# One gate product of a two-layer encoder from seven quarter products instead of eight

## The chip, the cores and the metric

The kernel runs on one core of a Trainium2 chip. A core has five engines with queues of their own: TensorE (PE in the profile, with its weight loads on a row of their own, PEld), VectorE (DVE), ScalarE (ACT), GpSimd (POOL) and SyncE (SP), which here only issues DMAs. The metric is the device time of one execution in microseconds, lower is better. Before the change it is 667.46 us, the median of three runs (667.1 to 667.55).

## The reference

The reference is an encoder trunk of two layers over 512 tokens with 1024 features, all in float32. Each layer has a token mixer, and after it the step that the change touches:

```python
h = x + y                                                     # y: output of the mixer
gate = jax.nn.sigmoid(rmsnorm(h, ple_norm[i]) @ ple_w_gate[i])  # (512x1024) @ (1024x1024)
x = h + gate * (p[i] @ ple_w_proj[i])
...
return rmsnorm(x, final_norm)                                 # after the second layer
```

Layer 0 mixes by neighbourhood attention, layer 1 by multi-head latent attention (MLA). `ple_norm` is scaled up by about 100, so the sigmoid's argument is large and small errors of the product can be seen in the output.

## The kernel before

**Precision.** No float32 matmul is used. Every operand is split in two: `hi`, a copy rounded to the matmul's type float32r (one ACT instruction), and `lo = x - hi` (one DVE or POOL instruction). A product is then the sum of three, hi by hi, lo by hi and hi by lo, all accumulated in one bank of PSUM (`mms`, `by_chunk`, L98 and L389). Activations are split by `split` (L87: ACT copy, DVE subtract), weights by `load_w` (L68: DMA from SP's queue into `wraw`, ACT copy into `whi` on L78, POOL subtract into `wlo` on L79).

**Tiling.** The 512 tokens are four blocks `t` of 128. A square product (1024 by 1024) is done in eight groups: two halves `n` of 512 output columns, and in each the four token blocks. One group is 24 matmuls of 128x128 by 128x512: eight slices of the contraction, three terms each. The weights of a half come as four chunks of 128x1024, each of which holds two slices.

**The second layer's last two products.** `out_proj` (L397) multiplies the attention's output `oT` by `mla_o`. DVE adds each group onto the residual rows `res[t]` (L409) and calls `turn_h` (L836): DVE multiplies the new half row by `ple_norm` (L839, `hg`), PE transposes it (L128), `split` makes `hnT[t]`, and after the second half ACT squares the row, DVE and POOL turn the sum into `rh[t]`, the inverse root mean square (L110 to L112). `gate_phase` (L465) multiplies `hnT` by the gate weights. Per group: ACT takes the sigmoid with `rh[t]` as its scale (L479), DVE multiplies by `pe` (L480; `pe` was computed earlier and is loaded from DRAM) and adds to `res[t]` (L482). `done` (L864) then gathers the sum of squares of the final norm, and in the half n = 0 POOL multiplies the row by the final gain (L879). When a row is complete, POOL raises to the power -1/2 (L882), DVE and ACT scale the two halves (L883, L884) and two DMAs write the row out. The very last group is done in two pieces of 256 columns.

**What sets the order.** The program is traced in the order of the source. A planner then puts each engine's instructions in order, the earlier in the source first among those that it takes to be ready, and hands out the buffers; the queues run in that order. So an instruction far down in the source can be queued early when its inputs are early, and one whose buffer is not free cannot. The buffers that matter here: three each of `wraw`, `whi` and `wlo`; five more pairs `whi`, `wlo` for the output and the gate product (`wxn` of L826); eight big buffers of 128x2048 (four hold `oT` until the output product is over, the other four `hnT`); two PSUM banks `mm`, two `S`, three `T`, one `O`; eight buffers `z` of 128x512, free once the attention is over; three of `pe`.

```python
    def load_w(self, ap, n, extra=False, parts=1, rest=None, late=None):   # L68
...
            nc.scalar.activation(hi[:, c], raw[:, c], AF.Copy)             # L78
            f = lambda e, c=c: e.tensor_tensor(out=lo[:, c], in0=raw[:, c], in1=hi[:, c].bitcast(F32), op=ALU.subtract)
```

Of the kernel before, what the change touches and what calls it, by code (L numbers as in the profile page):

```python
# [28 lines left out]
NWARM = 11  # L29
NLATE = 3  # L30
NEARLY = 7


def win(t, r0, r1, off, dims):
# [5 lines left out]
class Trunk:  # L40
    def __init__(self, tc, ctx, a, dbg=None):
        self.tc, self.nc, self.a = tc, tc.nc, a
        self.dbg = dbg or {}
        nc = self.nc
        ec = ctx.enter_context
        self.const = ec(tc.tile_pool(name="const", bufs=1))
        self.big = ec(tc.tile_pool(name="big", bufs=8))
        self.zp = ec(tc.tile_pool(name="zp", bufs=8))
        self.wp = ec(tc.tile_pool(name="wp", bufs=4))
        self.ps = ec(tc.tile_pool(name="ps", bufs=2, space=PSUM))  # L50
        self.ident = self.const.tile([P, P], F32, name="ident")
        self.half = self.const.tile([P, 1], F32, name="half")
        nc.vector.memset(self.half, -0.5)
        self.small = ec(tc.tile_pool(name="small", bufs=8))
        self.wx, self.wxn = None, 0
# [12 lines left out]
    def load_w(self, ap, n, extra=False, parts=1, rest=None, late=None):  # L68

        nc = self.nc  # L70
        pool = self.wx if extra else self.wp
        raw = self.wp.tile([P, 1024], F32, name="wraw", tag="wraw", bufs=3)
        hi = pool.tile([P, n if extra else 1024], F32R, name="whi", tag="whi", bufs=self.wxn if extra else 3)
        lo = pool.tile([P, n if extra else 1024], F32R, name="wlo", tag="wlo", bufs=self.wxn if extra else 3)
        w = n // parts
        for c in [slice(i * w, (i + 1) * w) for i in range(parts)]:
            nc.sync.dma_start(raw[:, c], ap[:, c])
            nc.scalar.activation(hi[:, c], raw[:, c], AF.Copy)  # L78
            f = lambda e, c=c: e.tensor_tensor(out=lo[:, c], in0=raw[:, c], in1=hi[:, c].bitcast(F32), op=ALU.subtract)  # L79
# [23 lines left out]
        return last  # L103


    def inv_rms(self, scratch, src, n):
# [4 lines left out]
        nc.vector.tensor_scalar(ss, ss, 1.0 / n, EPS, op0=ALU.mult, op1=ALU.add)  # L111
        nc.gpsimd.tensor_tensor(out=rs, in0=ss, in1=self.half, op=ALU.pow)  # L112
        return rs

    def rms(self, dst, src, g, n):
        rs = self.inv_rms(dst, src, n)
        self.nc.vector.scalar_tensor_tensor(dst, src, rs, g, op0=ALU.mult, op1=ALU.mult)

    def bcast(self, pool, ap, n, name, tag=None, bufs=None):
# [363 lines left out]
                    after(t, n, o, w)  # L483


    def mla_c(self, pool, xT, cT, sets):
        nc, a = self.nc, self.a
        tok = pool.tile([P, NT, 2, 16], F32, name="tok", tag="tok", bufs=1)
# [271 lines left out]
    def run(self):  # L760
# [7 lines left out]
        with tc.tile_pool(name="pre", bufs=4, reuse_waits="tile") as pool:  # L768
# [34 lines left out]
                nc.scalar.activation(xt[t], xt[t], AF.Square, accum_out=ss[:, t:t + 1])  # L803
            self.ple(pool, 0, "pe", 6, operands)
            nc.gpsimd.tensor_scalar(ss, ss, 1.0 / D, EPS, op0=ALU.mult, op1=ALU.add)
            nc.gpsimd.tensor_tensor(out=ss, in0=ss, in1=self.half.to_broadcast([P, NT]), op=ALU.pow)
            turned = self.transposes([ss[:, t:t + 1].to_broadcast([P, P]) for t in range(NT)])
            R = pool.tile([P, S], F32, name="R", bufs=1)
# [14 lines left out]
        x1T = None  # L823
        for layer in range(2):
            with tc.tile_pool(name=f"out{layer}", bufs=4, reuse_waits="tile") as pool:
                self.wx, self.wxn = pool, 5  # L826
                res = []
                for t in range(NT):
                    r = pool.tile([P, D], F32, name="r", tag="r")
                    nc.sync.dma_start(r, a["x"][t] if layer == 0 else self.spill[t])  # L830
                    res.append(r)
                gp = self.bcast(pool, a["ple_norm"][layer], D, "gp")
                gn = self.bcast(pool, a["norm_g"][1] if layer == 0 else a["final_norm"], D, "gn")
                hnT, rh = {}, {}

                def turn_h(t, n):  # L836

                    hg = pool.tile([P, S], F32, name="hg", tag="hg", bufs=3)
                    nc.vector.tensor_tensor(out=hg, in0=res[t][:, n * S:(n + 1) * S],  # L839
                                            in1=gp[:, n * S:(n + 1) * S], op=ALU.mult)  # L840
                    if n == 0:
                        hnT[t] = self.big.tile([P, 2 * KD, P], F32R, name="hnT", tag="big")
                    ps = self.transposes([hg[:, i * P:(i + 1) * P] for i in range(4)])
                    self.split(hnT[t][:, 4 * n:4 * n + 4, :], hnT[t][:, KD + 4 * n:KD + 4 * n + 4, :],
                               ps.rearrange("p (a b) -> p a b", a=4))
                    if n == 1:
                        sq = pool.tile([P, D], F32, name="sq", tag="xn", bufs=2)
                        rh[t] = self.inv_rms(sq, res[t], D)

                self.out_proj(a["na_o"] if layer == 0 else a["mla_o"], oT, res, turn_h, last)  # L850
                if layer == 0:
                    x1T = ([self.bigtile(f"x1h{g}") for g in range(2)], [self.bigtile(f"x1l{g}") for g in range(2)])

                    def done(t, n, o, w):
                        if n == 0:
# [3 lines left out]
                        self.rms(xn, res[t], gn, D)  # L859
                        self.rows_to_cols(xn, colsT(x1T, t))  # L860
                else:
                    mean = {}

                    def done(t, n, o, w):  # L864
                        c = slice(n * S + o, n * S + o + w)
                        r = res[t]
                        sq = pool.tile([P, D], F32, name="sq", tag="xn", bufs=2)
                        mn = self.small.tile([P, 1], F32, name="mn", tag="mn")
                        if c.start > S:
                            nc.vector.tensor_tensor_reduce(sq[:, :w], r[:, c], r[:, c], 1.0 / D, mean[t], op0=ALU.mult,  # L870
                                                           op1=ALU.add, accum_out=mn)
                        else:
                            ss = self.small.tile([P, 1], F32, name="ss", tag="ss")
                            nc.scalar.activation(sq[:, :w], r[:, c], AF.Square, accum_out=ss)
                            nc.vector.tensor_scalar(mn, ss, 1.0 / D, mean.get(t, EPS), op0=ALU.mult, op1=ALU.add)
                        mean[t] = mn
                        if c.stop < D:
                            if n == 0:
                                nc.gpsimd.tensor_tensor(out=r[:, c], in0=r[:, c], in1=gn[:, c], op=ALU.mult)  # L879
                            return  # L880
                        rs = self.small.tile([P, 1], F32, name="rs", tag="rs")
                        nc.gpsimd.tensor_tensor(out=rs, in0=mn, in1=self.half, op=ALU.pow)  # L882
                        nc.vector.scalar_tensor_tensor(r[:, S:], r[:, S:], rs, gn[:, S:], op0=ALU.mult, op1=ALU.mult)  # L883
                        nc.scalar.activation(r[:, :S], r[:, :S], AF.Copy, scale=rs)  # L884
                        nc.sync.dma_start(a["out"][t][:, S:], r[:, S:])
                        (nc.scalar if c.start > S else nc.sync).dma_start(a["out"][t][:, :S], r[:, :S])
                self.gate_phase(pool, layer, hnT, rh, res, done)
# [112 lines left out]
```

## Time and profile before

| | us |
|---|---|
| median of three runs | 667.46 |
| the profiled execution's span | 665.9 |
| what lies around the span, by the median | 1.6 |
| last weight split of the output product ends (POOL) | 596.1 |
| first matmul of the second gate | 614.1 |
| last matmul of the second gate ends | 658.6 |
| last instruction on DVE and ACT ends | 661.9 |

Times of the trace are counted from the start of the span. A row of the timeline gives start, duration, engine, line, operation, output and inputs; a row of the groups gives how many there are, their busy time, the mean duration in ns, and the idle time of the engine before them with what ended it. The profiled execution is the one that the prediction's sums are made against; its span and 1.6 us around it make the time of a run.

### The profile page before, as it was taken

What the parts mean: (1) busy time and instruction counts of PE and PEld (TensorE: products, weight loads), DVE (VectorE), ACT (ScalarE), POOL (GpSimd) and SP (SyncE); (2) the same over time, 40 slices, a digit from 0 to 9 for tenths busy, and PEclk for the clock granted to TensorE, in tenths of its full rate; (3) what the DMA queues carried; (4) which work ended last, traced back from release to release, by engine and by line L of the source; (5) the groups of instructions that cost most, each with busy time, mean ns of one, the idle gap of its engine ahead of it and who ended that gap; (6) DMA issues with size and microseconds to landing.
All of it is one profiled execution on the core that took longest, in us unless ns stands there. A gap on an engine that the chain in (4) does not pass through costs nothing.

```text
span 665.9 us, 9961 instructions
## 1 busy us (share of the span) xinstructions
PE 657.4 (99%) x3467; PEld 560.1 (84%) x3467; DVE 354.8 (53%) x794; ACT 407.9 (61%) x812; POOL 392.8 (59%) x320
## 2 busy tenths in 40 slices
PE   9999999999999999999999999999999999999995
PEld 6888888988988888888899888888888888888885
DVE  6280365736645514544625614888988875145234
ACT  7572586857767742543433635898979887436423
POOL 0395466575575765943044626786959786858410
PEclk9999999999999999999999999999999999999999
DMA  9944223222142236534233335120201223664022
GB/s 327 340 153 136 95 87 94 83 85 99 55 150 76 64 133 262 189 105 138 100 104 110 107 89 168 32 74 24 75 23 64 64 96 111 234 240 159 32 80 95
DMA packets 32386, 79.09 MB, mean 119 GB/s; under 512 B 4177, under 2 KB 8785, under 8 KB 32337
## 3 DMA queue, kind: packets, MB, share of 16 engines
q1 hardware_dynamic: 31904, 77.68, 35.0%
q10 hardware_dynamic: 432, 0.79, 0.3%
q8 instruction: 27, 0.44, 0.3%
q14 instruction: 23, 0.18, 0.1%
HBM read 66.92 MB, written 8.39 MB: 113 GB/s over the span
## 4 chain that ended last, share of the span: by engine, by line
PE 95%; DMA 1%; issue 1%; POOL 1%; DVE 0%; ACT 0%; SPq 0%; POOLq 0%; ACTq 0%
PE ps_mm L102 47%; PE ps_S L102 13%; PE ps_mm L550 6%; PE ps_T L128 6%; PE ps_O L661 4%; PE ps_T L102 3%; PE ps_O L102 3%; PE ps_T L227 2%; PE ps_O L383 2%; PE ps_mm L173 2%; PE ps_T L371 2%; PE ps_S L336 1%; PE ps_S L335 1%; PE ps_O L227 1%; DMA qe<-rl 1%
## 5 line engine op out<-in xcount | busy, mean ns | idle before, releaser
L79 POOL TENSOR_TENSOR wlo<-wraw,whi 128x1024 fp32r<-128x1024 f32 (+5 forms) x106 | 208.2, 1980 | 119.2 <-ACT whi L78 91.2
L78 ACT ACTIVATE whi<-wraw 128x1024 fp32r<-128x1024 f32 (+5 forms) x107 | 92.5, 886 | 86.9 <-PE ps_mm L102 17.8
L646 POOL TENSOR_TENSOR ex<-ex,rc 128x512 f32<-128x512 f32 x64 | 66.2, 1044 | 25.2 <-DVE rc L645 18.1
L102 PE MATMUL ps_mm<-whi,hnT 128*128 128x512 f32 (+1 forms) x272 | 70.2, 378 | 0.0
L102 PEld LDWEIGHTS ps_mm<-whi,hnT 128*128 128x128 f32 x272 | 49.3, 188 | 9.2
L644 ACT ACTIVATE ex<-ps_S,mx 128x512 f32<-128x512 f32 x64 | 44.0, 688 | 11.9 <-DVE mx L642 10.8
L642 DVE TENSOR_REDUCE mx<-ps_S 128x1 f32<-128x512 f32 x64 | 43.7, 683 | 6.9 <-PE ps_S L102 6.2
L91 DVE TENSOR_TENSOR pt_lo<-ps_T,pt_hi 128x512 fp32r<-128x512 f32 x64 | 43.3, 682 | 7.7 <-ACT pt_hi L89 7.3
L358 POOL TENSOR_TENSOR ex<-ex,rc 128x128 f32<-128x128 f32 (+1 forms) x64 | 34.1, 561 | 20.9 <-DVE rc L354 20.9
L102 PE MATMUL ps_mm<-xh,whi 128*128 128x512 f32 x152 | 40.8, 399 | 0.0
L102 PE MATMUL ps_mm<-wlo,hnT 128*128 128x512 f32 (+1 forms) x136 | 40.5, 378 | 0.0
L89 ACT ACTIVATE pt_hi<-ps_T 128x512 fp32r<-128x512 f32 x64 | 37.7, 594 | 4.4 <-PE ps_T L128 4.1
L128 PE MATMUL ps_T<-ident,ex 128*128 128x128 f32 x256 | 38.4, 272 | 0.0
L102 PE MATMUL ps_mm<-xl,whi 128*128 128x512 f32 x152 | 38.2, 390 | 0.0
L102 PE MATMUL ps_mm<-xh,wlo 128*128 128x512 f32 x152 | 38.0, 390 | 0.0
L128 PEld LDWEIGHTS ps_T<-ident,ex 128*128 128x128 f32 x256 | 31.5, 140 | 7.7 <-POOL ex L646 0.4
L102 PEld LDWEIGHTS ps_mm<-xl,whi 128*128 128x128 f32 x152 | 28.4, 188 | 5.8
L102 PEld LDWEIGHTS ps_mm<-xh,wlo 128*128 128x128 f32 x152 | 28.3, 188 | 5.8
L194 DVE TENSOR_TENSOR u<-ps_O,u 64x512 f32<-64x512 f32 x32 | 22.0, 687 | 19.9 <-ACT u L193 19.3
L112 POOL TENSOR_TENSOR rs<-ss,half 128x1 f32<-128x1 f32 x20 | 12.7, 637 | 33.7 <-DVE ss L111 33.6
L480 DVE TENSOR_TENSOR sg<-pe,sg 128x512 f32<-128x512 f32 (+1 forms) x17 | 12.4, 728 | 35.8 <-ACT sg L479 35.8
L352 ACT ACTIVATE ex<-ex,mx 128x128 f32<-128x128 f32 (+1 forms) x64 | 30.3, 474 | 1.9 <-DVE mx L342 1.0
(354 smaller groups left out, 1644.6 us busy)
## 6 DMA issues: line engine op xcount, KB each, us to landing
pe<-pe SPq DMA_DIRECT2D x32, 256.0 KB, 2.8
wraw<-na_qk SPq DMA_DIRECT2D x16, 512.0 KB, 3.3
wraw<-gate SPq DMA_DIRECT2D x16, 512.0 KB, 3.4
wraw<-na_v SPq DMA_DIRECT2D x8, 512.0 KB, 3.3
wraw<-na_o SPq DMA_DIRECT2D x8, 512.0 KB, 3.5
wraw<-mla_z SPq DMA_DIRECT2D x8, 512.0 KB, 3.5
wraw<-mla_o SPq DMA_DIRECT2D x8, 512.0 KB, 3.6
wraw<-na_z SPq DMA_DIRECT2D x6, 512.0 KB, 5.4
```

Source lines behind the costliest of these rows:

```text
L78: nc.scalar.activation(hi[:, c], raw[:, c], AF.Copy)
L79: f = lambda e, c=c: e.tensor_tensor(out=lo[:, c], in0=raw[:, c], in1=hi[:, c].bitcast(F32), op=ALU.subtract)
L89: self.last_copy = nc.scalar.activation(hi, src, AF.Copy, scale=scale)
L91: nc.vector.tensor_tensor(out=lo, in0=src, in1=hi.bitcast(F32), op=ALU.subtract)
L102: last = self.last_mm = nc.tensor.matmul(out, l, r, start=i == 0, stop=i == n - 1)
L128: self.last_mm = self.nc.tensor.transpose(t[:, i * P:(i + 1) * P], b, self.ident)
L352: self.last_exp = nc.scalar.activation(e, e, AF.Exp, scale=-1.0, bias=mx[:, qt:qt + 1], accum_out=sm[:, qt:qt + 1])
L358: nc.gpsimd.tensor_tensor(out=e, in0=e, in1=rc[:, qt:qt + 1].to_broadcast([P, e.shape[1]]), op=ALU.mult)
L550: self.last_mm = nc.tensor.matmul(PS[key], *terms[i], start=i == 0, stop=i == len(terms) - 1)
L642: nc.vector.reduce_max(mx, sp, axis=AX.X, negate=True)
L644: nc.scalar.activation(ex, sp, AF.Exp, bias=mx, accum_out=sm)
L646: nc.gpsimd.tensor_tensor(out=ex, in0=ex, in1=rc.to_broadcast([P, S]), op=ALU.mult)
```

## The change

In layer 1 the gate product is no longer made in eight groups of 24 matmuls. The 512x1024 matrix of activations is taken as four quarters (two token blocks by 512 features) A11, A12, A21, A22, and the weights as four quarters of 512x512, `E` and `F` (slices 0 to 3; left and right columns), `G` and `H` (slices 4 to 7). Seven products of sums of quarters stand for the eight quarter products (Strassen's scheme in Winograd's form). Each of the seven is two groups of 12 matmuls. Everything outside the seven is additions:

- `halves`, `keep_half`: for token blocks 0 and 1 the transposed half row is split as before (it is an operand of two products by itself), and ACT also keeps a float32 copy; for blocks 2 and 3 only the copy is kept.
- `mixes`: per pair of token blocks, four subtractions on DVE make the mixed activations, and each of five operands gets an ACT copy and a subtraction for `lo` (two on DVE, three on POOL).
- `gate_seven`: raw gate weights stay in SBUF, eight additions of 128x1024 on DVE make the mixed weights in place, and seven pairs of chunks are split (14 ACT copies; `lo` of eight on POOL, of six on DVE). The products' results are added and subtracted with intermediate tiles in the `z` buffers (mostly DVE from PSUM, two additions on POOL), and only then come sigmoid, `pe`, residual and `done`. The order of the products is 1, 5, 6, 3, 2, 7, 4; operands are prepared two products ahead; the banks `mm` and `S` alternate. The last group again has two pieces of 256 columns.
- The rows are scaled before they are mixed: the mean square of the layer's input row is kept (`keep`, one small POOL instruction per row), `row_scale` turns it into a factor, and `hg` is multiplied by that as well; the later inverse root mean square takes the factor into account (`scaled`).
- Buffers: the output product's and the gate's extra weights share one ring of twelve (`w4`) instead of five pairs; one buffer `xn` instead of two; no `sg`. `done` no longer takes it that n = 1 comes last. Layer 0 keeps `gate_phase`; its `x1T` buffers are asked for a little later in the source.

```diff
+SEVEN = (1,)
...
+        tags = ("w4", "w4") if extra and self.wxn > 10 else ("whi", "wlo")
...
+        if keep is not None:
+            nc.gpsimd.tensor_scalar(keep, ss, 1.0, None, op0=ALU.add)
...
+    def row_scale(self, layer):
+        m, s, a, b = self.rows[layer]
+        nc.gpsimd.tensor_tensor(out=s, in0=m, in1=self.half.to_broadcast([P, NT]), op=ALU.pow)
+        nc.vector.reciprocal(m, m)
+        nc.gpsimd.tensor_scalar(a, m, 1.0 / D, None, op0=ALU.mult)
+        nc.gpsimd.tensor_scalar(b, m, EPS, None, op0=ALU.mult)
...
+    def keep_half(self, t, n, ps):
+        if t < 2:
...
+            self.split(x[:, t, :], x[:, 2 + t, :], ps)
+        nc.scalar.activation(self.F[n].bitcast(F32)[:, t, :], ps, AF.Copy)
+
+    def mixes(self, i):
+        f = [x.bitcast(F32) for x in self.F]
+        a, b, c, d = f[0][:, i, :], f[1][:, i, :], f[0][:, 2 + i, :], f[1][:, 2 + i, :]
+        def operand(p, x, lo):
...
+            nc.scalar.activation(t[:, i, :], x, AF.Copy)
+            lo.tensor_tensor(out=t[:, 2 + i, :], in0=x, in1=t[:, i, :].bitcast(F32), op=ALU.subtract)
+        m = self.pool_x.tile([P, S], F32, name="mix", tag="hg", bufs=3)
+        nc.vector.tensor_tensor(out=m, in0=c, in1=d, op=ALU.subtract)
+        operand(5, m, nc.vector)
+        nc.vector.tensor_tensor(out=m, in0=a, in1=m, op=ALU.subtract)
+        operand(6, m, nc.vector)
+        nc.vector.tensor_tensor(out=b, in0=b, in1=m, op=ALU.subtract)
+        operand(3, b, nc.gpsimd)
+        nc.vector.tensor_tensor(out=a, in0=a, in1=c, op=ALU.subtract)
+        operand(7, a, nc.gpsimd)
+        operand(4, d, nc.gpsimd)
+
+    def gate_seven(self, pool, layer, rh, res, after):
...
+        ring = lambda k: (self.wp, ("wraw", "whi", "wlo"), 3) if k < 3 else (pool, ("w4", "w4", "w4"), self.wxn)
...
+        def parts(t, eng):
...
+            nc.scalar.activation(hi, t, AF.Copy)
+            eng.tensor_tensor(out=lo, in0=t, in1=hi.bitcast(F32), op=ALU.subtract)
...
+        def prep(p):
+            for c in range(2):
+                t = {1: E, 5: E, 6: E, 3: Hh, 2: G, 7: F, 4: E}[p][c]
+                if p in (5, 6, 7, 4):
+                    add(t, {5: F, 6: Hh, 7: Hh, 4: G}[p][c])
+                W[p].append(parts(t, nc.vector if c and p != 1 else nc.gpsimd))
...
+        def finish(t, n, src, o=0, wd=S, own=None):
+            nc.scalar.activation(sg, src, AF.Sigmoid, scale=rh[t])
...
+            nc.vector.tensor_tensor(out=sg, in0=pe, in1=sg, op=ALU.mult)
+            nc.vector.tensor_tensor(out=r, in0=r, in1=sg, op=ALU.add)
+            after(t, n, o, wd)
...
+        for k, p in enumerate((1, 5, 6, 3, 2, 7, 4)):
+            if k + 2 < len(order):
+                prep(order[k + 2])
+            for i in range(2):
...
+                    ps = self.psum(("mm", "S")[k % 2])[:, :wd]
+                    self.mms(ps, [(L(s, kk), R(r, kk)) for c in range(2) for s, r in ((0, 0), (1, 0), (0, 1))
+                                  for kk in (2 * c, 2 * c + 1)])
+                    if p == 1:    s1[i] <- ACT copy of ps
+                    elif p == 5:  y[i] <- ACT copy of ps
+                    elif p == 6:  w[i] <- DVE ps - s1[i];  y[i] <- POOL y[i] + w[i]
+                    elif p == 3:  DVE ps + y[i];   finish(i, 1)
+                    elif p == 2:  DVE ps + s1[i];  finish(i, 0)
+                    elif p == 7:  DVE w[i] - ps;  DVE y[i] - ps;  finish(2 + i, 1)
+                    else:         DVE ps - w[i];  finish(2 + i, 0)
...
-                self.wx, self.wxn = pool, 5
+                self.wx, self.wxn = pool, 11 + layer if seven else 5
```

(The last branch, per product, is written in short: one line for what are two to four calls in the diff.)

More of the change, by code (lines that the diff above doesn't have):

```diff
@@ L54, in __init__ @@
         self.small = ec(tc.tile_pool(name="small", bufs=8))
+        self.rows = [[self.const.tile([P, NT], F32, name=f"row{n}{l}") for n in "abcd"] for l in range(2)]
         self.wx, self.wxn = None, 0
@@ L834, in run @@
                 hnT, rh = {}, {}
+                if seven:
+                    self.row_scale(layer)
+                    self.halves(pool)
                 def turn_h(t, n):
                     hg = pool.tile([P, S], F32, name="hg", tag="hg", bufs=3)
[L839 to L841 removed]
+                    h, g = res[t][:, n * S:(n + 1) * S], gp[:, n * S:(n + 1) * S]
+                    if seven:
+                        nc.vector.scalar_tensor_tensor(hg, h, self.rows[layer][1][:, t:t + 1], g,
+                                                       op0=ALU.mult, op1=ALU.mult)
+                    else:
+                        nc.vector.tensor_tensor(out=hg, in0=h, in1=g, op=ALU.mult)
+                    if n == 0 and not seven:
@@ L850, in run @@
+                    if n == 1:
+                        if seven and t >= 2:
+                            self.mixes(t - 2)
+                        sq = pool.tile([P, D], F32, name="sq", tag="xn", bufs=2 - seven * layer)
+                        scaled = [x[:, t:t + 1] for x in self.rows[layer][2:]] if seven else None
+                        rh[t] = self.inv_rms(sq, res[t], D, scaled=scaled)
                 self.out_proj(a["na_o"] if layer == 0 else a["mla_o"], oT, res, turn_h, last)
+                seen = set()
```

139 lines of the change are left out of this document (115 added, 24 removed).

## The prediction

> **What bounds the kernel now.** I read the page's first two parts and the chain that ended last, then the windows of the stage that changes.
>
> ```profile
> span 665.9 us, 9961 instructions
> PE 657.4 (99%) x3467; PEld 560.1 (84%) x3467; DVE 354.8 (53%) x794; ACT 407.9 (61%) x812; POOL 392.8 (59%) x320
> PE   9999999999999999999999999999999999999995
> PE 95%; DMA 1%; issue 1%; POOL 1%; DVE 0%; ACT 0%; SPq 0%; POOLq 0%; ACTq 0%
> ```
>
> TensorE is busy 99% of the span and carries 95% of the chain: as the kernel stands, a matmul less is time less. The profiled span of 665.9 us and 1.6 us around it make the median of 667.46; I sum against the span and add the difference.
>
> ```profile
> 570.00:619.00 49.00, 49.00 (x232) 40.73 (x231) 16.53 (x28) 22.46 (x30) 37.97 (x21) 1.00 0.60 211
> 596.10:614.10 18.00, 18.00 (x88) 14.92 (x88) 6.91 (x13) 11.21 (x16) 15.65 (x10) 1.00 0.48 150
> 614.10:661.90 47.80, 44.47 (x221) 37.64 (x219) 18.71 (x37) 18.10 (x34) 14.22 (x12) 1.00 0.20 70
> ```
>
> The second gate's first matmul starts at 614.1 and the last DVE and ACT instructions end at 661.9. In these windows PE is full until the tail; DVE is busy 6.9 + 18.7 us, ACT 11.2 + 18.1, POOL 15.7 + 14.2 of 65.8. The share of DMA in the last is 0.20; I don't look for a bound there.
>
> **What the change takes from PE.** The sigmoid of a group starts as its 24 matmuls end:
>
> ```profile
> 625.72 0.69 ACT L479 ACTIVATE sg<-ps_mm,rs 128x512 f32<-128x512 f32 x1 [1.68 <-PE ps_mm L102]
> 631.16 0.69 ACT L479 ACTIVATE sg<-ps_mm,rs 128x512 f32<-128x512 f32 x1 [2.48 <-PE ps_mm L102]
> ```
>
> The distance of the two is 5.44 us for 24 matmuls, 227 ns each. Eight groups of 24 are 192 matmuls, seven products of 24 are 168: 24 fewer, **-5.44 us**. Transposes stay at four per half row. Nothing else leaves the path.
>
> **What it adds, by engine.** Durations from the groups between 596.2 and 662 us (the gate's work; from the left, count, busy us, mean ns):
>
> ```profile
> L79 POOL TENSOR_TENSOR wlo<-wraw,whi 128x1024 fp32r<-128x1024 f32 x8 | 19.5, 2465 | 0.2 <-ACT whi L78 0.2
> L879 POOL TENSOR_TENSOR r<-r,gn 128x512 f32<-128x512 f32 x4 | 5.1, 1281 | 14.8 <-ACT sq L874 14.8
> L480 DVE TENSOR_TENSOR sg<-pe,sg 128x512 f32<-128x512 f32 x7 | 4.8, 693 | 19.5 <-ACT sg L479 19.5
> L480 DVE TENSOR_TENSOR sg<-pe,sg 128x256 f32<-128x256 f32 x2 | 0.8, 425 | 0.6 <-ACT sg L479 0.6
> L839 DVE TENSOR_TENSOR hg<-r,gp 128x512 f32<-128x512 f32 x4 | 3.2, 790 | 0.1
> L883 DVE SCALAR_TENSOR_TENSOR r<-r,rs,gn 128x512 f32<-128x512 f32 x4 | 3.0, 752 | 2.1 <-POOL rs L882 2.0
> L870 DVE CUSTOM_DVE_ANT_0 sq<-r,mn 128x256 f32<-128x256 f32 x1 | 0.5, 486 | 0.0
> L91 DVE TENSOR_TENSOR hnT<-ps_T,hnT 128x512 fp32r<-128x512 f32 x5 | 3.4, 689 | 6.5 <-ACT hnT L89 6.5
> L78 ACT ACTIVATE whi<-wraw 128x1024 fp32r<-128x1024 f32 x7 | 7.3, 1055 | 2.1 <-DMA wraw<-gate 2.0
> L89 ACT ACTIVATE hnT<-ps_T 128x512 fp32r<-128x512 f32 x5 | 2.9, 590 | 1.6 <-PE ps_T L128 1.6
> ```
>
> DVE: 512 columns take 0.69 us and 256 take 0.42, so 1024 would take 0.69 + 2 x 0.27 = 1.23 us. The change adds eight weight additions (9.8 us), six weight `lo` (7.4), in `mixes` four subtractions and two `lo` for each of two pairs (12 x 0.69 = 8.3), eleven combinations out of PSUM and two of 256 columns (8.4), and drops the `lo` of two half rows (-1.4): +32.5 on 25.6, so 58.1 us. Without the 5.4 us of PE there are 65.8 - 5.4 = 60.4: DVE by itself just fits.
> ACT: six more weight copies (6.3 us), ten mixed operands, two net copies of half rows and four out of PSUM (16 x 0.59 = 9.4): 29.3 + 15.7 = 45.0, it fits.
> POOL: weight `lo` stay at eight, now spread over seven products; six mixed `lo` and two additions are 8 x 1.28 = 10.2: 29.9 + 10.2 = 40.1, it fits.
>
> By these sums each engine has room. They leave out that DVE and POOL stop each other. The timeline of both, where they subtract side by side early in the kernel and in the first output product:
>
> ```profile
> 38.58 4.72 POOL L817 TENSOR_TENSOR xl<-xT,xh 128x512 fp32r<-128x512 f32 x3
> 43.26 2.84 POOL L79 TENSOR_TENSOR wlo<-wraw,whi 128x1024 fp32r<-128x1024 f32 x1
> 39.39 7.26 DVE L817 TENSOR_TENSOR xl<-xT,xh 128x512 fp32r<-128x512 f32 x4
> ...
> 277.66 2.67 POOL L79 TENSOR_TENSOR wlo<-wraw,whi 128x1024 fp32r<-128x1024 f32 x1 [0.66 <-ACT whi L78]
> 277.38 3.50 DVE L839 TENSOR_TENSOR hg<-r,gp 128x512 f32<-128x512 f32 x2
> ...
> 31.03 4.77 POOL L79 TENSOR_TENSOR wlo<-wraw,whi 128x1024 fp32r<-128x1024 f32 x2 [6.00 <-ACT whi L78]
> 33.52 5.35 DVE L815 SCALAR_TENSOR_TENSOR xT<-ps_T,g,xT 128x512 f32<-128x512 f32 x8
> ```
>
> Four DVE subtractions with both inputs in SBUF, 0.69 us each elsewhere, take 7.26 us, because POOL runs the same kind from 38.58 to 46.10; the last of the four ends at 46.65, 0.55 after POOL's. At 277.38 two DVE multiplications take 3.50 us behind one POOL subtraction, which itself takes 2.67 instead of 2.39. L815, which has one input in PSUM, is not touched (eight in 5.35 us beside a running POOL). So such DVE and POOL instructions take turns, and the turns add up: from 38.58 to 46.65, 8.07 us, hold 3 x 1.28 + 2.39 + 4 x 0.55 = 8.43 us of them, so handing over saves 4%. A blocked DVE instruction takes 0.55 us of turn for 512 columns, 1.09 for 1024, 0.28 for 256.
>
> The Trainium skill, "SBUF — State Buffer", section "Who interferes with whom", has this as a rule: a DVE instruction with two SBUF inputs contends with a GpSimd instruction that reads SBUF, and the later one waits until the other is done. The trace agrees, 7.26 us instead of 2.8. By that rule POOL's small powers (two inputs in SBUF) would take turns too, eight by about 0.55 us.
>
> ```profile
> 374.99 1.06 POOL L112 TENSOR_TENSOR rs<-ss,half 128x1 f32<-128x1 f32 x2 [1.23 <-DVE ss L111]
> 375.57 0.62 DVE L117 SCALAR_TENSOR_TENSOR cn<-c,rs,gq 128x384 f32<-128x384 f32 x1
> ```
>
> Here a DVE multiplication of 384 columns starts under the second power and takes 0.62 us, no longer than its size asks for, so I count the powers at nothing; with them the sum below would be 4.4 us longer and the forecast, at the same 90%, 4.9 us higher.
>
> **The turns of the stage.** POOL is free of the output product's weights from 593.73 + 11.85/5 = 596.1 on:
>
> ```profile
> 593.73 11.85 POOL L79 TENSOR_TENSOR wlo<-wraw,whi 128x1024 fp32r<-128x1024 f32 x5 [1.60 <-ACT whi L78]
> 618.61 2.39 POOL L79 TENSOR_TENSOR wlo<-wraw,whi 128x1024 fp32r<-128x1024 f32 x1
> ```
>
> Before, POOL: 8 x 2.39 + 4 x 1.28 = 24.2 us; DVE: 4 of `hg`, 14 of L480 and L482, 4 of L883, 22 x 0.55 = 12.1, four of 256 columns 1.1, L870 0.3: 13.5. Together 37.7 of 65.8 us, so the turns hid beside PE. After: POOL +10.2; DVE 8 additions and 6 `lo` of 1024 columns 15.3, 12 in `mixes` 6.6: **37.7 + 32.1 = 69.8 us**, more than the 60.4 that PE would leave. The pair of DVE and POOL becomes the bound.
>
> How early can it begin? Before 614.1 only what needs no token block 2 or 3 and has a buffer: `lo` for products 1 and 5 (2 x 2.39 + 2.39 + 1.09), six additions (6.5), `hg` of three blocks (1.7), 16.5 us in the 18.0 from 596.1; the raw chunks come no earlier because their three `wraw` are the output product's. So the stretch can be full from the start, no more, and the remaining 53 us stand against 44.4 us of PE before and 39.0 after.
> How full does the pair stay? Upper end: as full as from 38.58 to 46.65, 69.8 x 8.07/8.43 = 66.8 us, ending at 662.9. Lower end: 570 to 619, where POOL was the busiest before: 37.97 less four powers (3.1) plus eight `hg` (4.4) is 39.3 of 49.0 us, 80%: 87.3 us, ending at 683.4. In the middle of the stage both queues hold work that is ready, like the first; before 614.1, and at the end, where each step waits for an ACT sigmoid or square, it is like the second. I take the middle, 90%: 77.6 us, ending at **673.7** instead of 661.9, **+11.8 us**.
>
> Where it shows: DVE's queue is in order, so the combinations out of PSUM stand behind blocked instructions, `mm` and `S` come free late, operands of products 6, 3 and 2 come late, and PE, with 38 us of work, waits. The finishing steps of the last products pile up on DVE behind the last matmul.
>
> **Small parts.** The tail:
>
> ```profile
> 658.61 0.47 ACT L479 ACTIVATE sg<-ps_mm,rs 128x256 f32<-128x256 f32 x1 [0.19 <-PE ps_mm L102]
> 659.12 0.43 DVE L480 TENSOR_TENSOR sg<-pe,sg 128x256 f32<-128x256 f32 x1 [0.45 <-ACT sg L479]
> 659.58 0.42 DVE L482 TENSOR_TENSOR r<-r,sg 128x256 f32<-128x256 f32 x1
> 661.19 0.75 DVE L883 SCALAR_TENSOR_TENSOR r<-r,rs,gn 128x512 f32<-128x512 f32 x1 [0.66 <-POOL rs L882]
> 661.94 0.38 ACTq L886 DMA_DIRECT2D out<-r  x1
> ```
>
> From the last matmul (658.6) to the last DMA's issue (661.9) the change adds a subtraction out of PSUM of 256 columns ahead of the sigmoid, 0.42 us and a handover of 0.19: +0.6, for the case that PE stays the bound; the output's 4 us after it are the same. Row scaling: `keep` puts one more POOL instruction ahead of the power in layer 0's rows.
>
> ```profile
> 23.73 0.19 POOL L805 TENSOR_SCALAR ssq<-ssq 128x4 f32<-128x4 f32 x1 [0.22 <-ACT x L803]
> ...
> 332.91 1.28 DVE L117 SCALAR_TENSOR_TENSOR x1n<-r,rs,gn 128x1024 f32<-128x1024 f32 x1
> 337.65 1.03 PE L128 MATMUL ps_T<-ident,x1n 128*128 128x128 f32 x8
> ```
>
> It costs about 0.19 us (L805); the last row's normalised values are there at 334.2 and PE turns them at 337.65, so it is hidden, and would cost 4 x 0.19 without that cover. `row_scale` is four small instructions with the attention of layer 1 to be run beside. SP's queue: the same eight weight loads, one `pe` load more; a load waits for its buffer, not for the queue. The copies and operands of the activations need nine big buffers of eight: the fifth operand waits for product 1's, which ends 5.4 us in; its first use is the last product. `xn` and the ring of twelve cost turns at most inside one engine.
>
> **The rivals.** (1) *PE stays the bound; faster.* It decides whether the turns of DVE and POOL fit in before PE is done: they would have to end by 657.1 + 0.6, within 61.6 us, so 8 us of the 69.8 would have to overlap or start before 596.1. Time 667.46 - 5.44 + 0.6 = **662.6**. For it: each engine's own sum fits, and the planner may queue weight work early. Against: handing over gave 0.36 us on 8.43, not 8 on 70. (2) *The pair is full all the time*: end 662.9 to 665.9 (with and without the 4%), **668.5 to 671.5**. For it: the stretch at 38.58; against: the ACT steps between. (3) *The pair is held up more, 80%*: **689**. For it: DVE queues waits for PE and ACT in front of ready work. (4) *The two cancel*, gain and tail, about 667.5.
>
> **How the numbers follow.** The likeliest case, 671.5 to 688 around 679: 0.64. (3), over 688: 0.08. (2): 0.08. (4): 0.04. (1): 0.16. A difference of 0.2% is about what a measurement of this kernel tells from none. Slower: 0.64 + 0.08 + 0.08 = 0.80; the same 0.04; faster 0.16. Time 667.46 + 11.8 = 679. The range leaves out most of (1) and what lies over 688: 665 to 688; the likeliest case's own range is 671.5 to 688.
>
> **What would show it.** Right: 24 matmuls fewer in the gate; PE with holes of together 15 us or more after 614, their releasers DVE or POOL; DVE's two-input subtractions and additions at means well over 0.69 and 1.23 us; DVE and POOL together near full; several us of DVE between the last matmul and the last DMA. Wrong: PE full to the end and means as before (then rival 1), or DVE's durations short and PE waiting for weight DMAs or for ACT.

## The result and the profile after

The changed kernel takes 683.48 us, the median of four runs (683.09 to 684.25), against 667.36 for the kernel before on the same chip: 1.0244 times the time, 95% interval 1.0231 to 1.0256, or 16.1 us more. The profiled execution's span is 681.7 us instead of 665.9.

The page of the changed kernel: span, busy times, two rows of the 40 slices, and the chain that ended last by engine.

```profile
span 681.7 us, 9979 instructions
...
PE 657.6 (96%) x3431; PEld 558.0 (82%) x3431; DVE 400.8 (59%) x830; ACT 423.2 (62%) x836; POOL 414.7 (61%) x336
...
PE   9999999999999999999999999999999999995891
...
PEclk9999999999999999999999999999999999997897
...
PE 88%; DVE 8%; issue 1%; POOL 1%; ACT 0%; DMA 0%; POOLq 0%; DVEq 0%; ACTq 0%
```

PE has 36 instructions fewer: 24 matmuls' worth of time, and 12 more because the last group, done in two halves of its columns, is now 12 matmuls and not 24. PE is as busy as before all the same (657.6 us, it was 657.4), so the matmuls that are left take longer; and the row of its clock is no longer all nines at the end. DVE has entered the chain with 8%.

The stage in windows (columns: width; busy us and instructions of PE, PEld, DVE, ACT, POOL; granted clock; share of DMA; GB/s):

```profile
596.10:614.10 18.00, 18.00 (x87) 14.95 (x86) 12.78 (x15) 8.99 (x13) 10.58 (x6) 1.00 0.36 140
614.10:661.90 47.80, 38.35 (x151) 30.08 (x150) 44.43 (x43) 26.14 (x41) 33.19 (x18) 0.86 0.05 17
...
622.00:627.00 5.00, 1.85 (x6) 0.93 (x6) 5.00 (x4) 3.05 (x6) 3.68 (x1) 0.64 0.00 0
627.00:632.00 5.00, 3.41 (x8) 2.76 (x9) 4.96 (x5) 1.54 (x3) 2.70 (x1) 0.50 0.00 0
...
646.00:662.00 16.00, 16.00 (x69) 13.15 (x68) 12.70 (x17) 6.58 (x12) 9.99 (x7) 0.96 0.14 50
```

From 614.1 to 661.9 DVE was busy 18.7 us before and is 44.4 now, POOL 14.2 and now 33.2; PE fell from 44.5 to 38.4 with only 151 matmuls in it instead of 221. All that PE waited for from 596 on (us in all, times, longest):

```profile
PE ps_T L137 <- ACT hf L518: 3.1, 1, 3.1
PE ps_S L105 <- DVE X L531: 2.9, 1, 2.9
PE ps_mm L105 <- DVE w L636: 2.6, 1, 2.6
PE ps_mm L105 <- DVE X L531: 2.1, 1, 2.1
PE ps_S L105 <- ACT X L530: 1.3, 1, 1.3
```

The costliest groups of DVE and POOL in the same stretch:

```profile
L565 DVE TENSOR_TENSOR wlo<-wr,whi 128x1024 fp32r<-128x1024 f32 x6 | 13.1, 2200 | 0.0
L572 DVE TENSOR_TENSOR wr<-wr 128x1024 f32<-128x1024 f32 x8 | 11.1, 1396 | 6.1 <-DMA wr<-gate 6.1
L531 DVE TENSOR_TENSOR X<-mix,X 128x512 fp32r<-128x512 f32 x4 | 4.8, 1228 | 0.0
...
L534 DVE TENSOR_TENSOR mix<-hf,hf 128x512 f32<-128x512 f32 x2 | 3.5, 1770 | 0.0
...
L565 POOL TENSOR_TENSOR wlo<-wr,whi 128x1024 fp32r<-128x1024 f32 x8 | 22.8, 2857 | 11.8 <-ACT whi L564 11.8
L531 POOL TENSOR_TENSOR X<-hf,X 128x512 fp32r<-128x512 f32 x6 | 10.7, 1801 | 2.6 <-ACT X L530 2.6
...
L121 POOL TENSOR_TENSOR rs<-ss,half 128x1 f32<-128x1 f32 x4 | 4.1, 1025 | 3.3 <-DVE ss L118 1.7 <-PE ps_mm L105 1.6
```

DVE's subtractions of 1024 columns take 2.20 us and those of 512 columns 1.23 to 1.77, where 1.23 and 0.69 were worked out for an instruction left alone. POOL's take 2.86 and 1.80 instead of 2.47 and 1.28. The timeline of PE and DVE (start, duration), with the first weight addition, the matmuls inside and after the slow clock, and the end of both engines:

```profile
600.81 3.62 DVE L572 TENSOR_TENSOR wr<-wr 128x1024 f32<-128x1024 f32 x3 [6.07 <-DMA wr<-gate]
...
630.46 1.91 PE L105 MATMUL ps_S<-whi,X 128*128 128x512 f32 x4
...
635.14 1.07 PE L105 MATMUL ps_S<-whi,X 128*128 128x512 f32 x4
...
670.08 0.40 PE L105 MATMUL ps_mm<-wlo,X 128*128 128x256 f32 x2
...
677.07 0.75 DVE L1056 SCALAR_TENSOR_TENSOR r<-r,rs,gn 128x512 f32<-128x512 f32 x1 [0.66 <-POOL rs L1055]
```

The last matmul ends at 670.5, 11.9 us later than before, and DVE's last instruction at 677.8: the tail between them is 7.3 us, it was 3.4. 11.9 + 3.9 is the 15.8 us of the span. Since 5.44 us of matmuls are gone, PE loses 17.3 us: 12.0 are the waits above, and the other 5.3 lie in matmuls that ran while the granted clock was down (four in 1.91 us at 630.46, in 1.07 at 635.14).

The chain that ended last (start, us, what), from 604.9 to the end, is DVE's for 56.5 of 72.8 us; PE stands in it for 6.0 us only:

```profile
642.40 3.42 PE ps_mm L105 x10
645.82 2.59 PE ps_S L105 x8
```

At 227 ns these 18 matmuls would take 4.1 us, so 1.9 of the 5.3 us that the low clock cost lie on the chain.

### The profile page after: what moved, and what is told of

Its sections match the earlier page's. It is cut to its first block, busy times and chain, and to the rows that moved or that the text cites. A ratio compares the mean times of both kernels' runs of the same rounds, so it can differ in the third digit from the quotient of the medians.

```text
span 681.7 us, 9979 instructions
## 1 busy us (share of the span) xinstructions
PE 657.6 (96%) x3431; PEld 558.0 (82%) x3431; DVE 400.8 (59%) x830; ACT 423.2 (62%) x836; POOL 414.7 (61%) x336
## 3 DMA queue, kind: packets, MB, share of 16 engines
q1 hardware_dynamic: 32048, 77.68, 33.2%
## 4 chain that ended last, share of the span: by engine, by line
PE 88%; DVE 8%; issue 1%; POOL 1%; ACT 0%; DMA 0%; POOLq 0%; DVEq 0%; ACTq 0%
PE ps_mm L105 41%; PE ps_S L105 13%; PE ps_mm L703 6%; PE ps_T L137 6%; PE ps_O L814 4%; PE ps_T L105 3%; PE ps_T L236 2%; PE ps_O L105 2%; PE ps_O L392 2%; PE ps_mm L182 2%; PE ps_T L380 2%; DVE wlo L565 1%; PE ps_S L345 1%; PE ps_S L344 1%; DVE wr L572 1%
## 5 line engine op out<-in xcount | busy, mean ns | idle before, releaser
L82 POOL TENSOR_TENSOR wwlo<-wraw,wwhi 128x1024 fp32r<-128x1024 f32 (+5 forms) x93 | 176.5, 1913 | 107.3 <-ACT wwhi L81 79.1
L81 ACT ACTIVATE wwhi<-wraw 128x1024 fp32r<-128x1024 f32 (+5 forms) x94 | 79.1, 863 | 74.4 <-issue 21.8
L797 ACT ACTIVATE ex<-ps_S,mx 128x512 f32<-128x512 f32 x64 | 44.0, 688 | 11.9 <-DVE mx L795 10.8
L105 PE MATMUL ps_mm<-xh,wwhi 128*128 128x512 f32 x152 | 40.8, 399 | 0.0
L105 PE MATMUL ps_mm<-xl,wwhi 128*128 128x512 f32 x152 | 38.2, 390 | 0.0
L105 PE MATMUL ps_mm<-xh,wwlo 128*128 128x512 f32 x152 | 38.0, 390 | 0.0
L105 PE MATMUL ps_mm<-wwhi,hnT 128*128 128x512 f32 x128 | 35.0, 392 | 0.0
L105 PEld LDWEIGHTS ps_mm<-xl,wwhi 128*128 128x128 f32 x152 | 28.4, 188 | 5.9
L105 PEld LDWEIGHTS ps_mm<-xh,wwlo 128*128 128x128 f32 x152 | 28.3, 188 | 5.8
L105 PE MATMUL ps_S<-ke,qe 96*128 96x512 f32 x96 | 28.9, 407 | 0.1
L105 PE MATMUL ps_S<-ko,qo 128*128 128x512 f32 x96 | 28.9, 409 | 0.0
```

Source lines behind the costliest of these rows:

```text
L105: last = self.last_mm = nc.tensor.matmul(out, l, r, start=i == 0, stop=i == n - 1)
L797: nc.scalar.activation(ex, sp, AF.Exp, bias=mx, accum_out=sm)
```

## The experiments

My theory: DVE and POOL take turns in instructions with two SBUF inputs (when both have one, one engine waits until the other is done), the pair is full, and PE waits for its late operands. The rivals: PE is still the bound; the order in the queues and not the turns makes the operands late; something that goes with the change (kept rows, buffers) costs; ACT or the weight loads hold it. Times of all runs stand against the kernel before on the same chip, 667.4 to 667.9.

**One SBUF input instead of two.** A bank of PSUM filled with zeros takes the place of one input, so that DVE's 26 instructions of weights and mixes no longer have two inputs in SBUF. The bank is freed by moving one group of the output projection from `O` to `T`. The first run has all of it, the next two the weights' 14 or the mixes' 12. What is left out is the second input itself, so the sums and differences are not formed. Parts of the edit:

```
-  ... ("mm", "mm", "S", "S", "T", "O", "mm", "mm")[n * NT + t]
+  ... ("mm", "mm", "S", "S", "T", self.ob, "mm", "mm")[n * NT + t]     # "T" in layer 1
...
+  self.zero = self.psum("O"); nc.vector.memset(self.zero, 0.0)
...
-  add = lambda x, y: nc.vector.tensor_tensor(out=x, in0=x, in1=y, op=ALU.add)
+  add = lambda x, y: nc.vector.tensor_tensor(out=two(x), in0=self.wide, in1=two(x), op=ALU.add)
```

> In the changed kernel, the weight additions and weight lo on DVE, and the subtractions and lo of mixes on DVE, take one input from a PSUM bank of zeros in place of the second SBUF input; same count, same sizes, the input that is made last is kept, so the order of the work stays. Left out: the differences and sums themselves, so the numbers that come out are others. (One transposing group of the output product moves from bank O to a T bank to free the bank.) Theory of turns (DVE with two SBUF inputs and POOL take turns): DVE's means fall to 0.69 and 1.23 us, and the 12 to 18 us of blocked time that these forms carry go; 665 to 672 us. Rival, DVE simply has too much work in its queue: the work is the same, 681 to 684 us.

> The same as the run before it, for the weight additions and the weight lo on DVE alone. Left out: those sums and differences. Theory of turns: about half of the gain, 674 to 679 us, since the trace shows 7 us of DVE's excess time on these lines and as much on those of mixes; and POOL's means fall with DVE's. Rival, too much work: 681 to 684 us.

> The same, for the subtractions and lo of mixes on DVE alone. Left out: those differences. Theory of turns: the other half, 674 to 679 us; if the mixed operands' chain is what PE waits for and the weights only stand by, more of the gain is here, 670 to 674. Rival, too much work: 681 to 684 us.

Measured: 686.5 us (ratio 1.0279, 1.0264 to 1.0294), 683.76 (1.0241, 1.0225 to 1.0256) and 682.48 (1.022, 1.0205 to 1.0236). What turns gave (665 to 672, and 674 to 679 for each part) is missed by all three; the second and third lie in the rival's 681 to 684, the first above it. A group of DVE in the first of them:

```profile
L570 DVE TENSOR_TENSOR wlo<-ps_O,whi 128x1024 fp32r<-128x1024 f32 x6 | 7.1, 1220 | 4.0 <-ACT whi L568 4.0
```

Its longest wait of PE:

```profile
PE ps_S L105 <- ACT whi L568: 11.6, 1, 11.6
```

And the sum of its four windows of 5 us from 597 to 617:

```profile
sum 20.00, PE 20.00 PEld 16.55 DVE 4.46 ACT 4.24 POOL 4.64; mean PE 5.00 PEld 4.14 DVE 1.11 ACT 1.06 POOL 1.16
```

The durations did what turns say, 2.20 us became 1.22. But DVE is busy 4.5 of 20 us from 597 to 617 (15.7 in the changed kernel), and PE then waits 11.6 us in one piece for the operands of the next product: with these operands the planner made another order. The other two runs have single waits of PE of 8.3 and 10.8 us that the changed kernel has not (both for `hg`). So the runs decide neither for turns nor for too much work, although two of them hit the rival's number: what the edit gained and what the new order cost can't be told apart. The edit had to be made with the order kept.

**Half of the matmuls.** `for kk in (2 * c, 2 * c + 1)` became `for kk in (2 * c,)` in the seven products, which leaves out half of their contraction.

> The changed kernel with every second slice of the contraction left out of the seven products: 84 matmuls of 512 columns fewer in time, 19 us of PE; every operand is still made and waited for. If the pair of DVE and POOL is the bound, PE's time is nearly free: 677 to 683 us, most of it where PE with a low granted clock stands in the chain. If PE is still the bound behind its waits: 664 to 668 us.

Measured: 680.87 us (1.0195, 1.0178 to 1.0212). 84 matmuls of 227 ns are 19.1 us, and the time falls by 2.6, inside the 677 to 683 of a bound that is not PE. The longest wait of PE:

```profile
PE ps_T L137 <- DVE hg L999: 8.0, 1, 8.0
```

The window of the stage:

```profile
614.10:661.90 47.80, 28.34 (x92) 19.76 (x90) 44.29 (x46) 26.65 (x40) 29.51 (x16) 0.75 0.06 21
```

DVE is as full as before, PE waits more and runs at a lower clock (0.75). PE is not the bound of the stage.

**The bank of zeros alone, and the same edit with the order held.** The control moves the one group to bank `S` and fills `O` with zeros that nobody reads. For the second run the instructions were noted as they were traced, and once the order, the buffers and the waits had been made, one input of each was replaced in place (written in short):

```
+  for n, i in enumerate(block.instructions):       # after the planner is done
+      kind, k = t.notes.get(i.name, ("", 0))       # 8 additions, 6 weight lo, 12 mixes of DVE
+      ins = list(i.ins); ins[k] = zero             # for 1024 columns: the bank read twice
+      block.instructions[n] = replace(i, ins=ins, outs=[i.outs[0]])
```

> The changed kernel; only one result bank of the output projection is another one and one DVE memset makes a bank of zeros that nobody reads. It is the kernel that the next two are held against: on ACT and POOL the order of the instructions is that of the changed kernel, on DVE too but for the memset. Both theories: 683.5 us, within 1 us. If it is off by more, the bank itself costs or gains something, and the first three experiments, which had such an edit in them, are read against that.

> As the kernel with the bank of zeros, with the same order on every engine and the same waits; after the order was made, one SBUF input of DVE's 8 weight additions, its 6 weight remainders and its 12 mixing operations was replaced by the bank of zeros, so these products are not the reference's. DVE then takes no turns with POOL in these 26 instructions. Theory of turns: DVE loses about 7 us in the weights and 7 us in the mixes (their excess over 1.23 and 0.69 each in the changed kernel), nearly all of it on the chain, so 669 to 676 us. Rival, that the order of the queues and the late operands set the end and the longer instructions only fill time that would be waited anyway: 681 to 684, as in the three experiments before, whose order had changed with the edit.

Measured: 683.34 us for the control (1.0236, 1.0221 to 1.0251), 673.47 with the edit (1.0087, 1.0072 to 1.0102). The sum of the control's windows from 596 to 682:

```profile
sum 86.00, PE 63.25 PEld 51.06 DVE 72.18 ACT 45.22 POOL 50.56; mean PE 12.65 PEld 10.21 DVE 14.44 ACT 9.04 POOL 10.11
```

The same of the run with the edit:

```profile
sum 86.00, PE 59.55 PEld 48.55 DVE 56.51 ACT 44.40 POOL 41.09; mean PE 11.91 PEld 9.71 DVE 11.30 ACT 8.88 POOL 8.22
```

The control is the changed kernel in time, and its trace has the changed kernel's order in this stage on DVE, ACT and POOL, but for the memset. The edited run lies inside the 669 to 676 of turns. With the same instructions in the same order, DVE is busy 15.7 us less and POOL, whose instructions weren't touched, 9.5 us less: that is what each waited for the other in these instructions. The run is 9.9 us shorter. Three groups of it:

```profile
L575 DVE TENSOR_TENSOR wlo<-ps_O,whi 128x1024 fp32r<-128x1024 f32 x6 | 7.2, 1216 | 2.4 <-ACT whi L574 2.4
L575 POOL TENSOR_TENSOR wlo<-wr,whi 128x1024 fp32r<-128x1024 f32 x8 | 19.4, 2436 | 12.8 <-ACT whi L574 11.1 <-PE ps_mm L106 1.7
...
L122 POOL TENSOR_TENSOR rs<-ss,half 128x1 f32<-128x1 f32 x4 | 2.2, 552 | 3.2 <-DVE ss L119 3.2
```

Even POOL's small powers (L122) take 0.55 us here and took 1.03 in the changed kernel: they had waited for DVE.

**POOL's wide instructions away.** The other side of the pair, in the same way: each noted POOL instruction gets 8 columns, and the matmuls that would read its remainder (the `lo` of a split) read `hi` columns of the activations. POOL's own work goes with the turns here, so this run by itself can't tell the two apart. In short:

```
+  narrow = lambda p: replace(p, ap=[p.ap[0], [1, 8]])
+  block.instructions[n] = replace(i, ins=[narrow(p) for p in i.ins], outs=[narrow(i.outs[0])])
```

> As the kernel with the bank of zeros, with the same order and the same waits; after the order was made, POOL's 20 wide instructions (8 weight remainders, 6 remainders of mixed operands, 2 additions, 4 products with the final gain) were cut to 8 columns each, and the 62 matrix products that would have read the 14 remainders read another part of the same operand, so the output is not the reference's. DVE then has no one to take turns with in the last stage and POOL's 42 us are gone. Theory of turns: all of DVE's excess of about 20 us goes, and what waited for POOL's remainders goes too: 662 to 671 us. Rival, DVE's own 58 us in this queue order and PE's waits for ACT set the end: 676 to 682.

Measured: 671.02 us (1.0053, 1.0036 to 1.007), 12.3 us under the control, at the upper end of what turns gave. DVE's two-input instructions are back at the lengths that they have alone, 1.22 us for 1024 columns and 0.68 for 512. PE's waits in this run:

```profile
PE ps_S L106 <- ACT X L539: 1.8, 1, 1.8
PE ps_S L106 <- DVE X L540: 1.3, 1, 1.3
```

Its chain from ACT's queue to PE's slow stretch:

```profile
619.87 0.48 ACT whi L574
...
620.84 0.95 ACT whi L574
...
621.82 2.36 DVE wlo L575 x2
624.18 0.61 DVE X L540
...
624.83 4.61 PE ps_S L106 x12
```

Its timeline: the first mixed tile, ACT's copy of it, and the ends of PE and DVE:

```profile
618.91 0.68 DVE L544 TENSOR_TENSOR mix<-hf,hf 128x512 f32<-128x512 f32 x1
...
622.12 0.67 ACT L539 ACTIVATE X<-mix 128x512 fp32r<-128x512 f32 x1
...
658.67 0.40 PE L106 MATMUL ps_mm<-wlo,X 128*128 128x256 f32 x2
...
664.29 0.75 DVE L1067 SCALAR_TENSOR_TENSOR r<-r,rs,gn 128x512 f32<-128x512 f32 x1 [0.66 <-POOL rs L1066]
```

This run is still 3.4 us over the kernel before, 3.0 in the span. Its tail is 6.0 us, 2.6 more than before, with no turns in it: DVE's own finishing steps. Its last matmul ends 0.5 us late in spite of 5.44 us less to do, and 5.0 of these 5.9 us can be seen: 3.1 us of waits for the first mixed operand, and 4.61 us for the twelve matmuls after them that take 2.72 at 227 ns. The mixed tile is ready at 619.6 and ACT copies it at 622.1; between the two it works off copies that stand ahead in its queue, of weights (`whi`) above all. The second wait is DVE's queue: two weight remainders, which had waited for those copies, stand ahead of the mixed operand's remainder (621.82 to 624.18 in the chain).

**DVE's additions away too.** The last run, with DVE's 8 weight additions narrowed as well.

> As the run with POOL's wide instructions cut (same order, same waits), and DVE's 8 weight additions cut to 8 columns too, 8 times 1.22 us of DVE's own time, so the output is not the reference's. That run's last matmul ended 0.5 us later than the kernel before's in spite of 24 matmuls fewer, with 3.1 us of PE waiting near 625 for the first mixed operands, and its end came 6 us after the last matmul. Theory, that DVE's own load is what is left: the hole closes and with it the low clock, 665 to 668 us. Rival, ACT (14.7 of 16 us busy from 614 to 630) makes the operands late: 669.5 to 671.

Measured: 670.44 us (1.0042, 1.0027 to 1.0057); the runs of the two overlap (669.76 to 671.22, and 670.18 to 672.18). Some 8.5 us of DVE's work are gone, as the group of the additions shows, and no gain can be told from it:

```profile
L583 DVE TENSOR_TENSOR wr<-wr 128x8 f32<-128x8 f32 x8 | 1.3, 161 | 8.2 <-DMA wr<-gate 5.3 <-POOL wlo L575 2.9
```

PE's longest wait is there as before:

```profile
PE ps_S L106 <- ACT X L539: 2.1, 1, 2.1
```

The rival holds: the hole stays, and ends with ACT's copy and then, after 0.8 us more, with DVE's remainder behind two of weights. By this account, once the turns are gone, the order of ACT's and DVE's queues from 620 to 624 and the tail keep the seven products from paying. No run closes the hole, and another order of these queues was not tried.

**What goes with the change.** `SEVEN = (1,)` became `SEVEN = ()`: kept row sums, row tiles and late allocation stay, the products are eight.

> The changed kernel with its list of layers that take seven products emptied: eight quarter products as before, but the kept row sums, the row tiles and the late allocation of the second layer's input stay. Both theories: 667.4 us within 0.7, nothing of these parts costs. If they cost, 668 to 672.

Measured: 667.65 us (1.0003, 0.9993 to 1.0012). They cost nothing. The row scaling itself, the ring of twelve and the single `xn` go with the seven products and were not run by themselves.

**The first experiment again, with the control's bank.** The edit on the inputs is in the source again, and the planner orders for itself.

> The edits of the first experiment (one input of DVE's 26 weight and mixing instructions is a bank of zeros), but the output projection's moved result bank is the one of the run with the idle zeros, and the planner orders the work for itself. With the order held the same edits gave 673.5. If the other bank made the first experiment slow (686.5): 672 to 676. If the order that the planner makes for these operands did: 680 to 687.

Measured: 679.26 us (1.0172, 1.0155 to 1.0189), between the two forecasts. One wait of PE shows why:

```profile
PE ps_S L105 <- ACT whi L568: 9.5, 1, 9.5
```

It is the wait of the first experiment, 2 us shorter, so the planner's order makes it with either bank. The same 26 edited instructions give 673.47 in the changed kernel's order, 679.26 in the planner's, and 686.5 in the planner's with bank `T`. The order, with the waits that the planner made for it, is 5.8 us here; the other 7.2 belong to bank `T` and the order that came with it, which these runs don't separate.

**Two versions that compute everything.** All 14 remainders that POOL made go to DVE (`nc.gpsimd` became `nc.vector` in `prep` and for products 3, 7 and 4 in `mixes`); and, in the other version, the mixed tile in PSUM (`m = self.psum("O")`, the projection's group in bank `S`).

> The changed kernel with all 14 remainders of the last gate that POOL made given to DVE; the planner orders anew. DVE's own sum is then 58.1 + 8 x 1.22 + 6 x 0.69 = 72.0 us, about what DVE was busy in the changed kernel with its waiting for turns, and POOL has only 6 wide instructions left. Theory of a full DVE: 678 to 684, no gain to speak of. Rival, that POOL's slow remainders (2.86 us each) held the products: 670 to 676.

> The changed kernel with the mixed tile kept in a PSUM bank that is free by then (the output projection's one group that used it takes another), all that is computed kept: 8 of the 12 mixing instructions then have at most one SBUF input or write none back; the planner orders anew. Theory of turns: two thirds of the mixes' 7.4 us of excess go, 678 to 680. If the new order costs as it did in the first three experiments: 681 to 687.

Measured: 678.29 us (1.0157, 1.0142 to 1.0172) and 679.44 (1.0176, 1.0161 to 1.0191). A group of the first:

```profile
L565 DVE TENSOR_TENSOR wlo<-wr,whi 128x1024 fp32r<-128x1024 f32 x14 | 16.9, 1229 | 2.2 <-POOL ww L82 1.3 <-ACT whi L564 0.9
```

A group of the second:

```profile
L532 DVE TENSOR_TENSOR X<-ps_O,X 128x512 fp32r<-128x512 f32 x4 | 2.7, 682 | 2.0 <-ACT X L531 2.0
```

In the first DVE's weight remainders are not held up any more, 1.23 us each, but there are 14 of them, and most of what DVE gained in turns it has in work (68.7 us busy from 596 to 682, where the changed kernel has 72.2); in the second the remainders of the mixes fall from 1.23 to 0.68 us. They save 5.2 and 4.0 us of the changed kernel's 16, and neither comes near the kernel before. The second is as forecast. The first lies at the lower edge of its 678 to 684, for which the forecast had said no gain to speak of.

## Why the prediction was right, and where it was short

The forecast was 679, in a likeliest case of 671.5 to 688; it is 683.5. Point by point:

- *PE loses 24 matmuls, 5.44 us.* Right, and worth nothing, as the forecast had it: 19.1 us more of matmuls taken away gave 2.6. The rival that PE stays the bound (662.6) is out.
- *DVE and POOL take turns, and the pair becomes the bound.* Right, and shown in an unchanged order: -9.9 us when DVE's instructions have one SBUF input, with all the work still there. Cutting POOL's instructions gives -12.3, turns and POOL's own work together. The Trainium skill, "SBUF — State Buffer", section "Who interferes with whom", has the rule that the forecast rested on; the trace agrees, 2.20 us against 1.22.
- *90% full, so the stage ends at 673.7.* This is the term that was mis-sized: 69.8 us of turns from 596.1 to 677.8 are 85%, still inside the forecast's two ends (80%, and 8.43 us of turns in 8.07). The start was not what was missing: DVE's first addition came only at 600.8, after a wait for a weight load, but POOL was at its remainders from 596.0. By the rows of the two timelines, neither engine was in a wide two-input instruction for 1.9 us up to 614.1 and 1.3 from there to 646; the other 6.8 of 10.0 us come after 646. There the products and the finishing follow one another: PE is full from 646 to 662 (16.00 of 16) with products that had come late, while DVE is busy 12.7 and POOL 10.0, and then the tail follows. That PE is full does not make it the bound again, since the chain leaves it at 648.4. One sum over the stage does not see these steps one after the other.
- *Powers count at nothing.* Right as far as the runs show. Four took 1.03 us instead of 0.55, but that is POOL's wait behind DVE, not a turn taken from DVE. In the run with POOL's wide instructions cut the powers are all still there, and DVE's two-input instructions keep their own lengths (1.22 and 0.68 us); one that began 0.32 us into a power of 0.55 took 0.69. The rule of the Trainium skill's page just named, which the forecast set aside for the powers, would have put it at 684; that this is near 683.5 is luck, since the powers cost DVE nothing that can be seen. No run is without them.
- *PE's holes of 15 us or more, released by DVE or POOL.* Measured: 12.0 us of waits, 7.6 of them ended by DVE and 4.4 by ACT, which the forecast had among the signs against it. The chain that ended last goes through DVE in these stretches too, so ACT is not what they hang on. The other 5.3 us are matmuls at a lower clock, which the forecast did not have at all. It saw PE's loss as waits alone.
- *Finishing steps pile up behind the last matmul.* Right: a tail of 7.3 us instead of 3.4; 2.6 of the 3.9 remain without POOL's wide instructions.
- *Row scaling, kept sums and buffers hidden.* Right for what could be left in place with eight products: 667.65. For the rest it is not shown.
- *The first rival's condition.* The forecast adds its 0.6 us twice there (657.1 has it already); the turns would have had to end 0.6 us earlier. Nothing else hangs on it.

Left open: which order of ACT's and DVE's queues would be best for seven products, and what a kernel without the holes in PE would get back of the clock's loss.

## What to carry to other kernels

Before matmuls are traded for additions, add up the two-input work of DVE and POOL together and not for each engine by itself: here each had room by its own sum and the pair had not. Look also at where the prepared operands stand in the in-order queues of the engines that make them; the same edited instructions cost 673.5, 679.3 or 686.5 us by order and bank. To test a cause in a planned kernel, change the instruction after the order has been made; an edit ahead of it tests the planner too.

## What the runs showed of the hardware that was not expected

PE's clock can fall after waits of 3.1 us and less, and takes time to come back. In the run with POOL's instructions cut, PE waited 1.8 and 1.3 us with two matmuls between; the window behind the waits:

```profile
625.00:629.00 4.00, 4.00 (x11) 3.14 (x12) 3.97 (x7) 3.49 (x6) 1.47 (x3) 0.57 0.00 0
```

Two rows of its timeline:

```profile
626.33 1.91 PE L106 MATMUL ps_S<-whi,X 128*128 128x512 f32 x4
...
630.64 1.07 PE L106 MATMUL ps_S<-whi,X 128*128 128x512 f32 x4
```

The granted clock is 0.57 from 625 to 629, and four matmuls take 1.91 us and not 1.07. In the changed kernel one wait was enough: the 2.1 us for DVE's `X` that ended at 642.40, with PE at work since 628.6. Its window, and four matmuls in it:

```profile
642.00:647.00 5.00, 4.60 (x14) 3.65 (x15) 4.87 (x4) 2.05 (x3) 5.00 (x3) 0.69 0.00 0
...
643.43 1.53 PE L105 MATMUL ps_mm<-whi,X 128*128 128x512 f32 x4
```

After the wait of 2.6 us that ended at 668.79 no slow matmul followed in the 1.7 us that PE still worked (0.40 us at 670.08 for two of 256 columns, as at 665.04). So the length of one wait does not decide it in these traces.

The Trainium skill, "TensorE: Matmul & The Clock Gate", section "What's actually happening", says that the clock is halved after an idle window of some 3.4 us and comes back after a busy one of as much. The halving agrees (1.91 against 1.07 us, 0.50 in the window from 627 to 632 of the changed kernel); no single wait in these two traces was as long as 3.4 us, so the page's figure is not a length of a gap that is safe.
